# Numbers, gates and y rows of the gathered tokens placed through DRAM by GpSimd's queue, and expert transposes three pairs later

## The chip, the cores and the metric

The program runs on one core of a Trainium2 chip. The metric is the device time of one execution in microseconds, the median of several runs. The engines are TensorE (PE, matmuls; its weight loads are listed as PEld), VectorE (DVE), ScalarE (ACT), GpSimd (POOL) and SyncE (SP). Every engine takes its own queue of instructions in order. Transfers (DMA) are issued from the queues of SP, ACT or POOL and are carried out by 16 transfer engines that all issuers share.

## The reference

One decoder layer for 256 tokens of width 1024 in float32. First a mixer (linear attention and block-sparse attention, with a residual), then a retrieval of experts. The change touches only the second half:

```
xn = rmsnorm(x, norm2_w)
q  = (xn @ w_query).reshape(T, 8, 2, 128)            # 8 heads, two halves
s  = einsum('thpd,hpkd->thpk', q, subkeys)           # 128 keys per half
sv, si = top_k(s, 16)
cand    = sv[..., 0, :, None] + sv[..., 1, None, :]  # 256 candidates
top_s, pos = top_k(cand, 16)
expert  = take_along_axis(si0 * 128 + si1, pos)      # one of 16384
gate    = softmax(top_s)
act     = gelu(einsum('thkd,td->thk', u_tab[expert], xn))
out     = x + einsum('thk,thkd->td', gate * act, v_tab[expert])
```

Each token so has 8 x 16 = 128 experts, each with a row of 1024 floats in u_tab and one in v_tab.

## The kernel before

**Two ways for the experts.** The last 168 tokens ("many") go the dense way: TensorE multiplies their normed activations `yf` with the whole table u, 128 experts at a time (L120, 64 pairs `jp` of two pieces of 512 KB each), a gelu follows on ScalarE (L840), the gates are spread over all 16384 experts by products of one-hot rows (`one_hots`, `grid_group`, L808, from pair 31 on, `J0`), and TensorE multiplies with the whole table v (L881, again 64 pairs) into banks `acc`. The first 88 tokens ("few", `NS`) go by gathering: GpSimd's indirect transfer (L743) brings 128 rows of a table, one to each partition, and VectorE multiplies them with the token's normed row `y` and sums (L751, for u), or scales them by gate times gelu and adds them up in `ys` (L761, for v). There are 88 gathers from u and then 88 from v, through five buffers `rowsof`. A gather `k` takes its 128 row numbers from column `k` of the tile `ixs`.

**Three layouts.** `FEW = ((0, 64, 2), (64, 16, 8), (80, 8, 16))`: tokens 0 to 63 are spread over 2 blocks of 64 partitions each, tokens 64 to 79 over 8 blocks of 16, tokens 80 to 87 over 16 blocks of 8. So the y rows, the rstd, the expert numbers and the gates, which are computed with one token per partition, have to be copied to 2 + 8 + 16 = 26 places each. All these copies are transfers issued from ScalarE's queue, `parts_of` for numbers (`ixs`) and gates (`gs`), and the loop in `rows_of_few` for y rows (`ys`, L568) and rstd (`rs`, L569):

```python
for l, (t0, n, m) in enumerate(FEW):
    for b in range(m):
        nc.scalar.dma_start(ys[l][b * n:(b + 1) * n], rows_x2[t0:t0 + n])
        nc.scalar.dma_start(rs[b * n:(b + 1) * n, l:l + 1], rstd2[t0:t0 + n, 0:1])
```

**The stages.** From about 145 to 227 us TensorE computes the queries (16 pieces of w_query, L69 to L71, three matmuls each because each factor is split into two rounded parts). A piece comes by SP's queue into five `raw` buffers (L94), ScalarE rounds it (L100), VectorE computes the remainder (L101), and TensorE needs both; there are three buffers of each. In the same stage x2 is turned to rows (`x2_rows`), normed (`norm2`), and the y rows are placed (`rows_of_few`). From 227 us come the 64 pairs of u, then the 64 of v. Weight pieces are loaded ahead through a ring of 14 buffers.

**The order.** The search for the top 16 and what follows it is a list `work` of closures with costs, one list per half of the tokens. `work[0]` (tokens 0 to 127) is drained at 4.8 us of cost per pair, `work[1]` is spread over the pairs up to `J0 - 1`. What a closure leaves for TensorE, the transposes `turn` (L645) and `turn_gates` (L684), is put into `later` and issued in the next pair, behind its 16 matmuls. `few_to` spreads the 176 gathers over the pairs. This order of the program is not yet the order of the queues: the program is built with `schedule_with_timeline_sim=True` (L963), a planner that plays the program through with its own costs for operations and transfers, and puts an instruction into its engine's queue when its inputs are there in that plan. On the chip the order of each queue is then fixed. After pair 63 of v, L898 adds the residual to `acc`, L892 adds up the gathered sums `ys` on TensorE, and L893 adds their residual.

Of the kernel before, what the change touches and what calls it, by code (L numbers as in the profile page):

```python
# [9 lines left out]
F32 = mybir.dt.float32  # L10
# [8 lines left out]
D = 1024  # L19
# [6 lines left out]
J0 = 31  # L26
# [9 lines left out]
def layer(ctx: ExitStack, tc: tile.TileContext, a):  # L36
# [10 lines left out]
    def bank(tag):  # L47
        return psum.tile([128, 512], F32, name=tag, tag=tag, bufs=4 if tag == "sc" else 2)
# [464 lines left out]
    ixs = keep.tile([128, NS], U32, name="ixs")  # L513
    gs = keep.tile([128, NS], F32, name="gs")
    hs = keep.tile([128, NS], F32, name="hs")
    rs = keep.tile([128, 3], F32, name="rs")

    sums = act_p.tile([128, len(FEW), NS], F32, name="sums")
    gp.memset(sums, 0.0)
# [19 lines left out]
    spillT = nc.dram_tensor("x2_cols", (128, NC, ND), F32, kind="Internal").ap()  # L539
    rows_x2 = nc.dram_tensor("x2_rows", (NS, D), F32, kind="Internal").ap()  # L540

    def x2_rows(tt):
        x2 = tk.tile([128, D], F32, name="x2")
        for hf in range(2):
            p = bank("tr")
            for c in range(4):
                pe.transpose(p[:, c * 128:(c + 1) * 128], x2T[:, 4 * hf + c, tt * 128:(tt + 1) * 128], ident)
            ve.tensor_copy(x2[:, hf * 512:(hf + 1) * 512], p)
            junk = tk.tile([128, 512], BF, name="junk", tag="junk")
            sc_.activation(junk, x2[:, hf * 512:(hf + 1) * 512], AF.Square, accum_out=ss2[:, tt, hf:hf + 1])  # L550
        if tt == 0:
            nc.scalar.dma_start(rows_x2, x2[0:NS])
        gp.tensor_tensor(rstd2[:, tt:tt + 1], ss2[:, tt, 0:1], ss2[:, tt, 1:2], op=OP.add)

    def norm2():
        nc.scalar.dma_start(spillT, x2T[:, :, NS:])
        rstd_of(rstd2, D, NT)
        row = as_row(tk, rstd2, "rrow2")
        for c in range(NC):
            ve.scalar_tensor_tensor(yf[:, c], x2T[:, c, NS:], n2[:, c:c + 1], row[:, NS:], op0=OP.mult, op1=OP.mult)  # L560

    def rows_of_few():

        n2b = tk.tile([128, D], F32, name="x2")
        nc.scalar.dma_start(n2b, a["n2b"])
        for l, (t0, n, m) in enumerate(FEW):
            for b in range(m):
                nc.scalar.dma_start(ys[l][b * n:(b + 1) * n], rows_x2[t0:t0 + n])  # L568
                nc.scalar.dma_start(rs[b * n:(b + 1) * n, l:l + 1], rstd2[t0:t0 + n, 0:1])  # L569
            ve.scalar_tensor_tensor(ys[l], ys[l], rs[:, l:l + 1], n2b, op0=OP.mult, op1=OP.mult)  # L570


    scs = [tk.tile([128, NT, 4, 128], F32, name=f"scs{b4}") for b4 in range(4)]
# [4 lines left out]
    ij = tk.tile([128, 2, NT, 8, 16], F16, name="ij")  # L578
    cands = [tk.tile([128, 8, 112], F32, name="cand") for _ in range(NT)]
    later = []  # L580

    def top16(vals, idx, src):
        ve.max(vals[:, 0:8], src)
# [51 lines left out]
    def slots3(tt, w, eq):  # L635
        n = 8
        while n > 1:
            ve.tensor_tensor(eq[:, :, 0:n], eq[:, :, 0:n], eq[:, :, n:2 * n], op=OP.add)
            n //= 2
        ve.tensor_tensor(ij[:, w, tt], eq[:, :, 0], eq[:, :, 1], op=OP.add)  # L640
        later.append(lambda: turn(tt, w))

    def turn(tt, w):
        p = bank("tr").bitcast(F16)
        pe.transpose(p[:, :128], ij[:, w, tt].rearrange("p h k -> p (h k)"), identh)  # L645
        src, ts = many(tt, p)
        sc_.copy(idxT[:, w, ts], src[:, :, None].to_broadcast([128, ts.stop - ts.start, 2]))

    def parts_of(dst, src):

        for t0, n, m in FEW:
            w = SLOTS // m
            for b in range(m):
                nc.scalar.dma_start(dst[b * n:(b + 1) * n, t0:t0 + w], src[t0:t0 + n, b * w:(b + 1) * w])  # L654

    def experts():

        num = tk.tile([128, SLOTS], U32, name="num")
        r, c = (ij[:, w, 0].rearrange("p h k -> p (h k)") for w in range(2))
        numf = tk.tile([128, SLOTS], F32, name="numf")  # L660
        ve.scalar_tensor_tensor(numf, c, 128.0, r, op0=OP.mult, op1=OP.add)
        ve.tensor_copy(num, numf)
        parts_of(ixs, num)

    def gates(tt):
        gt = top[:, tt]
# [5 lines left out]
    def gates2(tt):  # L672
        gt = top[:, tt]
        sm = tk.tile([128, 8], F32, name="sm")
        ve.tensor_reduce(sm, gt, AX.X, OP.add)
        ve.reciprocal(sm, sm)
        ve.tensor_tensor(gt, gt, sm[:, :, None].to_broadcast([128, 8, 16]), op=OP.mult)
        if tt == 0:
            parts_of(gs, gt.rearrange("p h k -> p (h k)"))
        later.append(lambda: turn_gates(tt))  # L680

    def turn_gates(tt):
        p = bank("tr")
        pe.transpose(p[:, :128], top[:, tt].rearrange("p h k -> p (h k)"), ident)  # L684

        src, ts = many(tt, p)
        full = tk.tile([128, 128], F32, name="full")[:, :ts.stop - ts.start]
        g16 = tk.tile([128, 128], F16, name="g16")[:, :ts.stop - ts.start]
        sc_.activation(full, src, AF.Copy, scale=GS)
        sc_.copy(g16, full)  # L690
        sc_.copy(gf[:, 0, ts], g16)
        ve.tensor_tensor(gf[:, 1, ts], full, g16, op=OP.subtract)
# [128 lines left out]
    left1 = sum(c for c, _ in work[1])  # L821
    all1, spent = left1, 0.0
    for jp in range(64):
        pv = bank("mm")[:, :2 * ND].rearrange("p (k t) -> p k t", k=2)
        turns, later = later, []
        for k in range(2):
            by_col_whole(pv[:, k], take(("u", jp), k), yf)
        for f in turns:
            f()
        if jp == J0:  # L830
            assert not work[1] and not later
            tk_ctx.close()
            actB_p = ctx.enter_context(tc.tile_pool(name="actB", bufs=1))
            act[1] = actB_p.tile([128, 64, ND], F32, name="actB")
            oh = ctx.enter_context(tc.tile_pool(name="oh", bufs=2))
            one_hots(0)
        o = act_at(2 * jp, 2 * jp + 2)
        T = 4 * done_q
        if T < ND:
            sc_.activation(o[:, :, T:], pv[:, :, T:], AF.Gelu)  # L840
        if T:
            gl = oh.tile([128, 2, ND], F32, name="gl", bufs=1)
            sc_.activation(gl[:, :, :T], pv[:, :, :T], AF.Gelu)
            ve.tensor_tensor(o[:, :, :T], o[:, :, :T], gl[:, :, :T], op=OP.mult)
        if work[0]:
            spent -= 4.8
            while work[0] and spent < 0:
                c, f = work[0].pop(0)
                spent += c
                f()  # L850
            j1 = jp + 1
        else:
            few_to((jp - j1 + 1) * 2 * NS // (64 - j1 + 61))
            while work[1] and all1 - left1 < all1 * (jp + 1 - j1) / (J0 - 1 - j1):
                c, f = work[1].pop(0)
                left1 -= c
                f()
        while jp > J0 and done_q < NQ and done_q * (62 - J0) < (jp - J0) * NQ:
            grid_group(done_q, 2 * jp + 2)
            done_q += 1  # L860
            if done_q % 2 == 1 and done_q + 1 < NQ:
                one_hots(done_q + 1)
# [106 lines left out]
```

## Time and profile before

| what | value |
|---|---|
| median of 3 runs | 874.9 us (874.48 to 876.65) |
| the profiled execution | 877.12 us, span 875.3 us, mean granted clock 0.962 |
| busy | PE 823.0 us, DVE 482.1, ACT 247.3, POOL 215.1 |
| moved | 261.67 MB, mean 299 GB/s |
| chain that ended last | PE 82%, DVE 7%, DMA 5%, ACT's queue 3% |

The page gives the busy time of each engine, then 40 equal slices of the span with the busy share of each engine in tenths, the clock that TensorE was granted, and the traffic. Views of the trace give the same for any stretch of time, for one line of the program or one tile, and list who waited for whom. The span leaves out 1.8 us of the profiled execution's time.

### The profile page before, as it was taken

What the parts mean: (1) busy time and instruction counts of PE and PEld (TensorE: products, weight loads), DVE (VectorE), ACT (ScalarE), POOL (GpSimd) and SP (SyncE); (2) the same over time, 40 slices, a digit from 0 to 9 for tenths busy, and PEclk for the clock granted to TensorE, in tenths of its full rate; (3) what the DMA queues carried; (4) which work ended last, traced back from release to release, by engine and by line L of the source; (5) the groups of instructions that cost most, each with busy time, mean ns of one, the idle gap of its engine ahead of it and who ended that gap; (6) DMA issues with size and microseconds to landing.
All of it is one profiled execution on the core that took longest, in us unless ns stands there. A gap on an engine that the chain in (4) does not pass through costs nothing.

```text
span 875.3 us, 14841 instructions
## 1 busy us (share of the span) xinstructions
PE 823.0 (94%) x5734; PEld 777.0 (89%) x5734; DVE 482.1 (55%) x1060; ACT 247.3 (28%) x660; POOL 215.1 (25%) x252
## 2 busy tenths in 40 slices
PE   9999999928997499999999999999999999999995
PEld 6876689828997399999999999999999999999993
DVE  4795367494899644446666777645455445410003
ACT  5556345403220211019677776200000000000000
POOL 4141103000001833323222232433333333300000
PEclk9997899967999699999999999999999999999998
DMA  9453027814976899999999999999999999999701
GB/s 340 167 167 121 25 79 229 248 45 139 328 236 222 301 403 409 408 409 408 400 339 360 367 352 382 349 408 408 409 409 408 409 408 409 409 409 354 234 2 48
DMA packets 75551, 261.67 MB, mean 299 GB/s; under 512 B 10433, under 2 KB 12497, under 8 KB 75353
## 3 DMA queue, kind: packets, MB, share of 16 engines
q1 hardware_dynamic: 44883, 162.87, 50.0%
q0 software_dynamic: 25344, 92.29, 27.4%
q10 hardware_dynamic: 5254, 5.57, 2.3%
q8 instruction: 45, 0.74, 0.3%
q14 instruction: 25, 0.20, 0.1%
HBM read 258.50 MB, written 2.10 MB: 298 GB/s over the span
## 4 chain that ended last, share of the span: by engine, by line
PE 82%; DVE 7%; DMA 5%; ACTq 3%; ACT 1%; issue 1%; POOL 1%; SPq 0%; DVEq 0%
PE sc L881 31%; PE mm L120 28%; PE mm L71 4%; PE mm L69 4%; PE mm L70 4%; DMA raw<-in_v_rows 2%; PE tr L808 2%; ACTq L654 1%; PE sc L388 1%; ACTq L569 1%; PE mm L892 1%; ACTq L568 1%; DMA xT<-in_xT 1%; DMA ixs<-num 1%; PE sc L369 1%
## 5 line engine op out<-in xcount | busy, mean ns | idle before, releaser
L120 PE MATMUL mm<-yf,raw 128*128 128x168 f32 x1184 | 175.8, 307 | 0.0
L120 PEld LDWEIGHTS mm<-yf,raw 128*128 128x128 f32 x1184 | 169.5, 190 | 0.4 <-DMA raw<-in_u 0.4
L761 DVE SCALAR_TENSOR_TENSOR ys<-rowsof,hs,ys 128x1024 f32<-128x1024 f32 x85 | 109.1, 1284 | 101.6 <-DMA rowsof<-in_v_rows,ixs 101.4
L743 POOL DMA_INDIRECT rowsof<-in_u_rows,ixs x88 | 93.5, 1062 | 276.5 <-DVE hs L751 152.6
L751 DVE CUSTOM_DVE_ANT_0 junkd<-rowsof,ys 128x1024 bf16<-128x1024 f32 x88 | 107.5, 1222 | 48.8 <-DMA rowsof<-in_u_rows,ixs 47.9
L743 POOL DMA_INDIRECT rowsof<-in_v_rows,ixs x88 | 84.8, 964 | 147.2 <-DVE ys L761 125.7
L797 ACT ACTIVATE B<-E,gf 128x128 f16<-128x128 f16 x336 | 102.1, 388 | 22.3 <-PE tr L808 16.3
L881 PEld LDWEIGHTS sc<-actB,raw 128*128 128x128 f32 x608 | 87.1, 190 | 3.2 <-DMA raw<-in_v_rows 2.2
L881 PE MATMUL sc<-actB,raw 128*128 128x168 f32 x608 | 89.8, 307 | 0.1
L101 DVE TENSOR_TENSOR lo<-raw,hi 128x1024 fp32r<-128x1024 f32 x48 | 58.9, 1233 | 47.4 <-ACT hi L100 47.4
L881 PE MATMUL sc<-actA,raw 128*128 128x168 f32 x576 | 82.9, 306 | 0.0
L881 PEld LDWEIGHTS sc<-actA,raw 128*128 128x128 f32 x576 | 82.3, 190 | 0.0
L100 ACT ACTIVATE hi<-raw 128x1024 fp32r<-128x1024 f32 x48 | 50.4, 1057 | 67.2 <-PE mm L71 21.8
L120 PEld LDWEIGHTS mm<-yf,hi 128*128 128x128 f32 x432 | 63.3, 193 | 3.1 <-ACT actA L840 3.1
L120 PE MATMUL mm<-yf,hi 128*128 128x168 f32 x432 | 65.9, 311 | 0.1
L120 PE MATMUL mm<-yf,lo 128*128 128x168 f32 x432 | 64.8, 307 | 0.0
L120 PEld LDWEIGHTS mm<-yf,lo 128*128 128x128 f32 x432 | 62.1, 190 | 0.0
L69 PE MATMUL mm<-qhi,hi 128*128 128x256 f32 x128 | 38.7, 303 | 15.1 <-ACT hi L100 15.0
L898 DVE TENSOR_TENSOR x2d<-x2d,sc 128x504 f32<-128x504 f32 (+1 forms) x3 | 1.9, 619 | 91.1 <-PE sc L881 91.1
L840 ACT ACTIVATE actA<-mm 128x336 f32<-128x336 f32 x32 | 14.3, 450 | 105.3 <-PE mm L120 85.7
L71 PE MATMUL mm<-qhi,lo 128*128 128x256 f32 x128 | 38.6, 304 | 4.7 <-DVE lo L101 4.7
L69 PEld LDWEIGHTS mm<-qhi,hi 128*128 128x128 f32 x128 | 26.6, 208 | 15.6 <-ACT hi L100 15.6
(266 smaller groups left out, 1181.6 us busy)
## 6 DMA issues: line engine op xcount, KB each, us to landing
raw<-in_u SPq DMA_DIRECT2D x74, 512.0 KB
raw<-in_v_rows SPq DMA_DIRECT2D x74, 512.0 KB
hi<-in_u SPq DMA_DIRECT2D x27, 512.0 KB
lo<-in_u SPq DMA_DIRECT2D x27, 512.0 KB
hi<-in_v_rows SPq DMA_DIRECT2D x27, 512.0 KB
lo<-in_v_rows SPq DMA_DIRECT2D x27, 512.0 KB
raw<-in_w_rows SPq DMA_DIRECT2D x20, 512.0 KB
raw<-in_w_q SPq DMA_DIRECT2D x16, 512.0 KB
```

Of the source, the lines that this page charges most:

```text
L69: pe.matmul(ps, sh, mh, start=first, stop=False)
L70: pe.matmul(ps, sh, ml, start=False, stop=False)
L71: pe.matmul(ps, sl, mh, start=False, stop=last)
L100: sc_.activation(hi, raw, AF.Copy)
L101: ve.tensor_tensor(lo, raw, hi.bitcast(F32), op=OP.subtract)
L120: pe.matmul(ps, rv[:, c], mov[:, c], start=(c == 0), stop=(c == NC - 1))
L743: gp.indirect_dma_start(g, None, a[name], bass.IndirectOffsetOnAxis(ap=ixs[:, k:k + 1], axis=0))
L751: ve.tensor_tensor_reduce(junk, g, ys[place[k]], 1.0, 0.0, OP.mult, OP.add, hs[:, k:k + 1])
L761: ve.scalar_tensor_tensor(sumS, g, hs[:, k:k + 1], sumS, op0=OP.mult, op1=OP.add)
L797: sc_.activation(B[:, k], E[:, k], AF.Copy, scale=gf[:, m, 4 * q + k:4 * q + k + 1])
L808: pe.matmul(pv[:, k], A[:, k], B[m][:, k], start=(m == 0), stop=(m == 1))
L881: pe.matmul(acc[c // 3][:, c % 3], raw[:, c * 128:(c + 1) * 128], act[j // 64][:, j % 64], start=False, stop=j == NEXP - 1 and c in (2, 5, 7))
```

## The change

The y rows are scaled once, in token order (`yrow`), and `to_parts` writes them to DRAM and reads them back with one transfer per layout, three reads instead of 26 copies; the same for the numbers and the gates. All of these are issued by GpSimd's queue. The rstd column is no longer copied. The row copy of x2, its spill and the norm weights go from ScalarE's to SP's queue. The transposes of numbers and gates are due three pairs after the pair in which they are filed, and `work[1]` is spread over the pairs up to `J0 - 4`.

```diff
-    rs = keep.tile([128, 3], F32, name="rs")
+    xrow = tk.tile([128, D], F32, name="yrow")
     def x2_rows(tt):
-        x2 = tk.tile([128, D], F32, name="x2")
+        x2 = tk.tile([128, D], F32, name="x2") if tt else xrow
...
-            nc.scalar.dma_start(rows_x2, x2[0:NS])
+            nc.sync.dma_start(rows_x2, x2[0:NS])
     def norm2():
-        nc.scalar.dma_start(spillT, x2T[:, :, NS:])
+        nc.sync.dma_start(spillT, x2T[:, :, NS:])
+    def to_parts(dst, name, src, cols):
+        there = nc.dram_tensor(name, (NS, src.shape[1]), src.dtype, kind="Internal").ap()
+        gp.dma_start(there, src)
+        for l, (t0, n, m) in enumerate(FEW):
+            rows = there[t0:t0 + n]
+            if cols:
+                rows = rows.rearrange("t (m w) -> m t w", m=m)
+            else:
+                rows = rows[None].to_broadcast([m, n, src.shape[1]])
+            gp.dma_start(dst(l), rows)
+    def by_part(dst):
+        return lambda l: dst[:, FEW[l][0]:FEW[l][0] + FEW[l][1]]
     def rows_of_few():
         n2b = tk.tile([128, D], F32, name="x2")
-        nc.scalar.dma_start(n2b, a["n2b"])
-        for l, (t0, n, m) in enumerate(FEW):
-            for b in range(m):
-                nc.scalar.dma_start(ys[l][b * n:(b + 1) * n], rows_x2[t0:t0 + n])
-                nc.scalar.dma_start(rs[b * n:(b + 1) * n, l:l + 1], rstd2[t0:t0 + n, 0:1])
-            ve.scalar_tensor_tensor(ys[l], ys[l], rs[:, l:l + 1], n2b, op0=OP.mult, op1=OP.mult)
+        nc.sync.dma_start(n2b, a["n2b"])
+        yrow = xrow
+        ve.scalar_tensor_tensor(yrow[0:NS], xrow[0:NS], rstd2[0:NS, 0:1], n2b[0:NS], op0=OP.mult, op1=OP.mult)
+        to_parts(lambda l: ys[l], "y_rows", yrow[0:NS], False)
...
-        later.append(lambda: turn(tt, w))
+        later.append((at + 3, lambda: turn(tt, w)))
...
-        parts_of(ixs, num)
+        to_parts(by_part(ixs), "experts", num[0:NS], True)
...
-            parts_of(gs, gt.rearrange("p h k -> p (h k)"))
-        later.append(lambda: turn_gates(tt))
+            to_parts(by_part(gs), "gates", gt[0:NS].rearrange("p h k -> p (h k)"), True)
+        later.append((at + 3, lambda: turn_gates(tt)))
...
     for jp in range(64):
+        at = jp
-        turns, later = later, []
+        turns, later = [f for d, f in later if d <= jp], [x for x in later if x[0] > jp]
...
-            while work[1] and all1 - left1 < all1 * (jp + 1 - j1) / (J0 - 1 - j1):
+            while work[1] and all1 - left1 < all1 * (jp + 1 - j1) / (J0 - 4 - j1):
```

## Rows read from the trace of the kernel before

**Rows 1.** The page: busy time, TensorE in 40 slices, traffic in the same slices.

```profile
PE 823.0 (94%) x5734; PEld 777.0 (89%) x5734; DVE 482.1 (55%) x1060; ACT 247.3 (28%) x660; POOL 215.1 (25%) x252
...
PE   9999999928997499999999999999999999999995
...
GB/s 340 167 167 121 25 79 229 248 45 139 328 236 222 301 403 409 408 409 408 400 339 360 367 352 382 349 408 408 409 409 408 409 408 409 409 409 354 234 2 48
```

**Rows 2.** Windows: length, busy us (instructions) of PE, PEld, DVE, ACT, POOL; clock, DMA share, GB/s.

```profile
165.00:200.00 35.00, 14.77 (x99) 14.17 (x97) 26.24 (x141) 7.11 (x11) 0.00 (x0) 0.73 0.29 86
...
200.00:227.00 27.00, 26.14 (x192) 25.56 (x193) 16.87 (x59) 8.76 (x11) 0.00 (x0) 0.85 0.57 187
...
276.00:298.00 22.00, 5.07 (x33) 4.36 (x32) 16.58 (x25) 1.10 (x4) 14.21 (x10) 0.67 0.80 259
...
298.00:310.00 12.00, 12.00 (x77) 12.00 (x78) 8.11 (x16) 4.57 (x10) 8.41 (x8) 0.90 0.93 331
```

**Rows 3.** Waits of TensorE, 165 to 300 us: total, times, longest.

```profile
PE tr L645 <- ACT full L689: 16.4, 1, 16.4
...
PE mm L69 <- ACT hi L100: 15.0, 1, 15.0
...
PE mm L71 <- DVE lo L101: 4.7, 2, 4.0
...
PE tr L645 <- DVE ij L640: 1.1, 2, 0.7
```

**Rows 4.** ScalarE in order of time: start, length, what, count, idle before.

```profile
198.76 2.00 ACT L100 ACTIVATE hi<-raw 128x1024 fp32r<-128x1024 f32 x2 [12.77 <-DMA rs<-rstd]
...
278.01 17.06 ACTq L654 DMA_DIRECT2D ixs<-num  x24
```

**Rows 5.** Tiles rs, ys, ixs, issues: ns min/median/max, first and last start.

```profile
L569 ACTq DMA_DIRECT2D rs<-rstd x26: 497/638/708, 164.6 to 198.1; - x26
...
L568 ACTq DMA_DIRECT2D ys<-x_rows x26: 308/472/615, 158.6 to 197.6; - x26
...
L654 ACTq DMA_DIRECT2D ixs<-num x26: 537/632/675, 276.7 to 294.4; - x26
```

**Rows 6.** Windows of TensorE alone, busy us (instructions), clock, DMA, GB/s.

```profile
210.00:227.00 17.00, 17.00 (x148) 1.00 0.64 204
```

**Rows 7.** TensorE in order of time, behind the second hole.

```profile
297.72 3.89 PE L120 MATMUL mm<-yf,hi 128*128 128x168 f32 x16
...
301.45 7.00 PE L120 MATMUL mm<-yf,lo 128*128 128x168 f32 x48
```

**Rows 8.** GpSimd in order of time, the first and the third gather.

```profile
281.05 2.02 POOL L743 DMA_INDIRECT rowsof<-in_u_rows,ixs  x1 [117.07 <-PE tr L645]
...
285.40 0.94 POOL L743 DMA_INDIRECT rowsof<-in_u_rows,ixs  x1 [0.31 <-issue]
```

**Rows 9.** Chain of waits: two landings of small transfers.

```profile
198.07 1.75 DMA rs<-rstd
...
287.14 5.92 DMA ixs<-num
```

**Rows 10.** Windows of VectorE, lines L751 (287 to 391), L761 (550 to 875).

```profile
287.00:304.50 17.50, 12.32 (x20) 0.61 0.91 309
...
304.50:391.00 86.50, 38.24 (x62) 1.00 1.02 405
...
550.00:855.00 305.00, 105.29 (x82) 1.00 0.92 358
...
855.00:875.00 20.00, 3.84 (x3) 0.89 0.15 52
```

**Rows 11.** VectorE in order of time, 740 to 875 us.

```profile
768.67 1.28 DVE L761 SCALAR_TENSOR_TENSOR ys<-rowsof,hs,ys 128x1024 f32<-128x1024 f32 x1 [1.29 <-DMA rowsof<-in_v_rows,ixs]
...
860.89 0.68 DVE L898 TENSOR_TENSOR x2d<-x2d,sc 128x504 f32<-128x504 f32 x1 [90.94 <-PE sc L881]
...
862.34 1.28 DVE L761 SCALAR_TENSOR_TENSOR ys<-rowsof,hs,ys 128x1024 f32<-128x1024 f32 x1
```

More of the change, by code (lines that the diff above doesn't have):

```diff
@@ L580, in layer @@
     later = []
+    at = 0
     def top16(vals, idx, src):
@@ L647, in turn @@
         sc_.copy(idxT[:, w, ts], src[:, :, None].to_broadcast([128, ts.stop - ts.start, 2]))
[L649 to L654, printed above, removed]
     def experts():
```

## The prediction

> **What bounds the kernel now.** I read the page first. TensorE is busy 94% of the span, and its slices are full except for holes in the ninth, tenth, thirteenth and fourteenth slice, while the GB/s line stands near 409 from about 330 us on [rows 1]. So the end is set by TensorE's own work plus the holes in it; whoever fills a hole shortens the program by the hole, unless the tail gets longer. I cut the stretch around the holes into windows [rows 2]. From 165 to 200 us TensorE works 14.8 of 35 us; from 276 to 298 it works 5.1 of 22. In both the granted clock falls (0.73 and 0.67), and it is still 0.85 and 0.90 in the windows behind. The waits name who ends the long idles: an activation on ScalarE both times, L100 (the rounding of a weight piece) for 15.0 us and L689 (a copy of the gates) for 16.4 us [rows 3]. What ScalarE did meanwhile stands in the queue itself: L100 starts at 198.76 behind a row of transfers, and before L689 there is one block of 24 issues of ixs that lasts 17.06 us [rows 4]. Each of the small transfers costs ScalarE's queue 0.47 to 0.64 us, 26 times each for the rows, rstd and numbers [rows 5], and as often for the gates. The first hole is 52 issues, some 29 us of issue time spread over 158 to 199; the second is 26 of ixs and the last gs.
>
> **Part 1, rows and rstd off ScalarE.** Removed: 26 x 0.47 + 26 x 0.64 = 28.9 us of issues on ScalarE [rows 5], three multiplications of 1.28 us on VectorE become one, the rstd transfers go. Added: on SP three issues (x2 rows, spill, norm weights), which I take at the same 0.5 to 0.6 us each; they wait there for x2, and weight loads stand behind them, but up to five loaded pieces lie ahead of TensorE. On POOL one write and three reads. POOL has nothing else to do until 281 [rows 8], so nobody is behind them. What TensorE gets back: the 291 instructions of 165 to 227 [rows 2], at the pace of full clock in the last window, 17.00/148 = 0.115 us [rows 6], are 33.4 us of work in 62 us. So 28.6 us is the upper bound. The lower bound is the named idles alone, 15.0 + 4.7 = 19.7 us [rows 3], if the low clock stayed. I take 25: the slow matmuls come right after the idle and go with it, while VectorE, with 43 us of work in those 62, now has it in 37 and will make some pieces wait.
>
> **Part 2, numbers and gates off ScalarE, transposes three pairs later.** Removed: 52 issues x 0.63 us [rows 5]. The 16.4 us idle goes, and two small waits of the transposes for VectorE, 1.1 us together [rows 3], are covered by three pairs of matmuls. The slow start also goes: 16 matmuls took 3.73 us between their start and the next row, the next 48 took 7.00, or 0.146 each; 3.73 - 16 x 0.146 = 1.4 us [rows 7]. Sum 18.9; between zero (a new wait takes over) and 18.9 I take 18.5. What is late next is the placing: the first issue of the numbers goes at 276.7 [rows 5], the first gather starts at 281.05 [rows 8] after two issues and their landing. Now it is a write, its landing, a read, its landing. A direct POOL transfer does not occur before; its issue lies between 0 and the 2.02 us of an indirect one, I take the 0.94 of the plain case [rows 8]. A landing took 1.75 to 5.92 us [rows 9], I take 2.3, nearer to the small one on quiet queues. So 2 x (0.94 + 2.3) = 6.5 us after num against 4.3: the gathers start about 2 us later (bounds -1 and +12).
>
> A rule speaks against POOL as issuer. The first gather took 2.02 us in GpSimd's queue, the third 0.94 [rows 8]. The Trainium skill ("SBUF — State Buffer", section "SBUF: two separate sides") says that a VectorE operation in a two-port mode locks GpSimd out and so stops it from writing descriptors, and that transfers issued from ScalarE or SP do not suffer. The two durations would fit it, but these rows do not show what VectorE did at either. By it four issues in the chain cost up to 1.08 us more each, some 4 us, one or two multiplies more in the sum of part 3.
>
> **Part 3, what comes back at the end.** Each gathered block of expert rows is followed by one operation on VectorE. The order on VectorE was written by the planner, and it can be read. Three of the last multiplies (L761) stand behind the first output sum L898, which waits for TensorE's last matmul. On the chip the one before them started at 768.67, and then VectorE idles for 91 us; the three then run at 862 to 866.6 with TensorE finished, and the last products wait for them [rows 11]. So in the plan the gathered rows land later than on the chip; the plan is bound by transfers from the first gather on. The counts bear this out. By L751 (two instructions for each multiply) and L761, 10 multiplies fall in the second hole, 31 from there to 391, the other 47 of the 88 in the rest of the u stage, then 82 to 855 and 3 in the tail [rows 10]. VectorE was idle over half of the last long window (105.3 of 305 us), so a planner that held the rows to be there would have put them earlier. The hole was in the plan too, since ten multiplies stand ahead of the copy that ends it. In the hole the gathers had the transfer engines to themselves. Without it TensorE in the plan is at the same pair about 17 us sooner, the weight stream takes its share, and the plan is at every later pair about ten gathers behind, one more for the later start. Nothing in the plan makes that up until the weight stream ends. So I expect 3 + 11 = 14 multiplies behind L898. On the chip each costs 1.28 us if its row is there, as in the tail now [rows 11], and 17.5/10 = 1.75 us if row and operation take turns [rows 10]. Five buffers are full, so I take 1.4: 11 x 1.4 = 15.5 us longer tail. Bounds: 0 (the slip is made up) to 20 x 1.5 = 30 (it slips twice as far).
>
> **Sum.** -25 - 18.5 + 15.5 = -28 us. The profiled execution took 877.1 (span 875.3 and 1.8 around it), so 849; the median of the runs is 2.2 lower, so 847.
>
> **Rivals.**
> 1. The tail stays (three multiplies behind). For it: on the chip the gathers are 91 us early, and a planner that models transfers a little faster would move all of them ahead. Against: the counts above. Time: 847 - 15.5 = 831.
> 2. The gathers are late at the first one-hots. VectorE takes its queue in order, and 41 multiplies stand ahead of the gates and one-hots at 391 [rows 10]. If all stay there, 41 x 86.5/31 = 114 us from about 290 end at 404, while TensorE comes there 18 us before 391, 31 us too early at worst. Once TensorE waits, gathers take 1.75 us instead of 2.8, so I count half: 14 us, 861. Against: the planner, too, sees no hole and puts about ten fewer ahead.
> 3. The first hole is only half filled: SP holds the norm weights back until x2 is free, VectorE's scaled row waits for them, and rounding of pieces stands behind it. Gain 10 instead of 25: 862. For it: VectorE's L101 already ends 4.7 us of idles [rows 3].
> 4. Slower. The multiplies behind L898 in VectorE's queue decide: place, the tail; price, 1.4 us each. The 43.5 us gained are spent at 31 more, that is 34 behind L898, and past that the time is over 877. This needs the plan to reckon the DRAM round trip some 20 x 2.8 = 56 us longer than the old placing, since it gives away a gather per 2.8 us. Time at 38: 847 + 24 x 1.4 = 881. I see no row for it; the nearest landing is 5.92 [rows 9].
> 5. No change. The issue time of 17.06 us in one block [rows 4] is what the change moves, and if it were small against the transfers nothing would be gained: 875. The Trainium skill ("DMA: Bandwidth & Descriptors", section "Issuing engines are not separate DMA queues") says just this, that several issuers save only issue time, usually small beside the transfer. The trace disagrees here: with 0.2 to 16 KB each, the issue is the cost.
>
> **How the numbers follow.** Forecast 0.52; rival 1 0.22; rival 2 0.10; rival 3 0.08; rival 4 0.05; rival 5 0.03. A measurement of this kernel tells 0.3%, 2.6 us, from no change; so faster 0.92, same 0.03, slower 0.05. The forecast's own range, with 19.7 to 28.6 for part 1 and 8 to 17 multiplies in the tail, is 838 to 856. The range of 8 in 10 takes in rival 1 whole with 2 us below, 829, and the nearer half of rivals 2 and 3, to 862.
>
> **What would show it.** Part 1: L100's wait gone, TensorE idle under 5 us between 145 and the first u matmul, which starts near 202 and not 227; a granted clock near 1.0 there. Part 2: no idle over 1 us in the u stage before the one-hots; the first gather 6 to 9 us after num. Part 3: between 10 and 18 L761 behind the first L898, and 17 to 25 us from TensorE's last accumulation to its last product. Three there means rival 1; an idle of TensorE before L808 means rival 2; waits for DVE lo in the query stage mean rival 3. The forecast is wrong if the tail is as short as before, or if ScalarE's holes come back under another name.

## The result, and the profile after

The changed kernel takes 850.5 us (median of 4 runs, 848.89 to 852.24), the kernel before in the same comparison 875.8 us (4 runs, 874.48 to 878.48). The ratio is 0.9708, with a 95% interval of 0.9674 to 0.9742. The forecast was 847 us. The profiled execution took 849.4 us, of which the span covers 847.6.

The page after, the same three lines as in [rows 1].

```profile
PE 811.7 (96%) x5734; PEld 768.1 (91%) x5734; DVE 478.9 (57%) x1058; ACT 248.0 (29%) x660; POOL 224.5 (26%) x264
...
PE   8999999999999999999999999999999999999932
...
GB/s 341 182 154 145 26 75 215 265 229 368 233 218 338 408 409 408 408 406 369 356 357 373 360 351 381 409 409 409 408 409 409 408 409 409 408 345 200 1 191 173
```

TensorE's busy time is 11 us less for the same 5734 instructions, and the two pairs of holes are gone from its slices; in place of them the last two slices are low (3 and 2). The slice of 1 GB/s shortly before the end had its like before (2 GB/s); new is the traffic of 191 and 173 GB/s behind it: the transfers stand still while TensorE finishes, and then run again.

Two of the windows of [rows 2], and the tail (length; busy us and instructions of PE, PEld, DVE, ACT, POOL; clock, DMA share, GB/s).

```profile
165.00:200.00 35.00, 35.00 (x295) 35.00 (x294) 35.00 (x187) 13.42 (x18) 1.95 (x3) 1.00 0.84 240
...
276.00:298.00 22.00, 22.00 (x156) 22.00 (x155) 9.87 (x16) 2.26 (x5) 8.27 (x9) 1.00 1.03 409
...
811.50:847.60 36.10, 6.87 (x9) 1.82 (x8) 22.83 (x21) 0.00 (x0) 15.33 (x12) 0.64 0.63 214
```

TensorE now works all of 165 to 200 at a granted clock of 1.00, the 2.4 GHz level, on 295 instructions instead of 99, and all of 276 to 298. VectorE is full too in the first window. The tail, 36 us, has 9 instructions of TensorE.

Its waits after, to be laid beside [rows 3] (total, times, longest), and below them a wait of the kernel before that lies outside the window of [rows 3].

```profile
PE mm L901 <- DVE ys L769: 24.2, 2, 14.1
PE mm L120 <- DMA raw<-in_u: 1.5, 1, 1.5
...
PE sc L71 <- DVE lo L101: 0.8, 1, 0.8
...
PE mm L120 <- ACT actA L849: 0.7, 1, 0.7
```

```profile
PE mm L892 <- DVE ys L761: 4.3, 1, 4.3
```

L100 and the copy of the gates are gone from the list. The longest idle is now that of the last products (L901, L892 before) for VectorE's multiplies: 24.2 us in two pieces, where it was 4.3 in one.

GpSimd in order of time, after: the three placings, the first gathers, and gathers in the tail ([rows 5, 8] are before).

```profile
161.44 0.82 POOL L566 DMA_DIRECT2D y_rows<-yrow  x1 [5.36 <-DVE yrow L583]
165.70 1.95 POOL L573 DMA_DIRECT2D ys<-y_rows  x3 [3.44 <-DMA y_rows<-yrow]
...
247.15 0.55 POOL L566 DMA_DIRECT2D experts<-num  x1 [14.01 <-DVE num L670]
251.47 1.94 POOL L573 DMA_DIRECT2D ixs<-experts  x3 [3.77 <-DMA experts<-num]
257.74 1.09 POOL L751 DMA_INDIRECT rowsof<-in_u_rows,ixs  x1 [4.33 <-issue]
...
260.41 0.94 POOL L751 DMA_INDIRECT rowsof<-in_u_rows,ixs  x1 [0.30 <-issue]
...
814.49 1.86 POOL L751 DMA_INDIRECT rowsof<-in_v_rows,ixs  x1 [1.26 <-DVE ys L769]
...
824.51 2.04 POOL L751 DMA_INDIRECT rowsof<-in_v_rows,ixs  x1 [0.30 <-DMA rowsof<-in_v_rows,ixs]
...
830.98 0.94 POOL L751 DMA_INDIRECT rowsof<-in_v_rows,ixs  x1 [0.30 <-issue]
```

One write and three reads stand where 26 issues stood, each time. A write takes 0.55 to 0.82 us of the queue, a read some 0.65, and the reads start 3.4 to 3.8 us after the end of the write's issue.

TensorE in order of time, after: first matmul of u, first matmul of v, and the end.

```profile
194.72 3.58 PE L120 MATMUL mm<-yf,raw 128*128 128x168 f32 x24
...
512.60 5.58 PE L890 MATMUL sc<-actA,raw 128*128 128x168 f32 x38
...
806.81 4.72 PE L890 MATMUL sc<-actB,raw 128*128 128x168 f32 x32
825.62 3.37 PE L901 MATMUL mm<-ys,sums 128*88 128x512 f32 x4 [14.08 <-DVE ys L769]
839.08 3.46 PE L901 MATMUL mm<-ys,sums 128*88 128x512 f32 x4 [10.09 <-DVE ys L769]
```

VectorE in order of time, after, from the last multiply ahead of the output sums ([rows 11] before).

```profile
716.83 1.28 DVE L769 SCALAR_TENSOR_TENSOR ys<-rowsof,hs,ys 128x1024 f32<-128x1024 f32 x1 [1.26 <-DMA rowsof<-in_v_rows,ixs]
810.15 0.68 DVE L907 TENSOR_TENSOR x2d<-x2d,sc 128x504 f32<-128x504 f32 x1 [92.03 <-PE sc L890]
810.74 1.28 DVE L769 SCALAR_TENSOR_TENSOR ys<-rowsof,hs,ys 128x1024 f32<-128x1024 f32 x1
...
812.94 6.56 DVE L769 SCALAR_TENSOR_TENSOR ys<-rowsof,hs,ys 128x1024 f32<-128x1024 f32 x5
...
837.74 1.29 DVE L769 SCALAR_TENSOR_TENSOR ys<-rowsof,hs,ys 128x1024 f32<-128x1024 f32 x1 [1.12 <-DMA rowsof<-in_v_rows,ixs]
```

The residual sum L907 (L898 before) waits 92.03 us for TensorE, and 17 multiplies (16 of L769 and one of L771, the first of a half) stand behind it. They run from 810.74 to 839.03, and the last products wait. Five of their rows lay ready in the buffers; the other twelve gathers had to wait until those buffers came free, GpSimd's queue for 92.97 us.

Where the time went, from the spans: 875.3 before, 847.6 after.

| stretch | before | after | difference |
|---|---|---|---|
| start to the first matmul of u | 227.05 | 194.72 | -32.3 |
| u stage, to the first matmul of v | 334.9 | 317.9 | -17.0 |
| v stage, to the end of TensorE's last accumulation | 300.3 | 298.9 | -1.4 |
| tail, to the end of the span | 13.0 | 36.1 | +23.1 |

Of the first row 3.3 us are not the change's: the query stage begins that much earlier, because the granted clock between 70 and 100 us was 0.83 in this execution and 0.72 in the one of before, with the same instructions there. The profiles of the experiments show 0.72 to 0.83 there whatever part of the change they hold. The spans differ by 27.7 us and the medians by 25.2: the profiled execution of the kernel before was 1.3 us over its median, the one after 1.1 under.

### The profile page after: what moved, and what is told of

The parts are those of the page before. It is cut to its first block, busy times and chain, and to the rows that moved or that the text cites. A ratio compares the mean times of both kernels' runs of the same rounds, so it can differ in the third digit from the quotient of the medians.

```text
span 847.6 us, 14723 instructions
## 1 busy us (share of the span) xinstructions
PE 811.7 (96%) x5734; PEld 768.1 (91%) x5734; DVE 478.9 (57%) x1058; ACT 248.0 (29%) x660; POOL 224.5 (26%) x264
## 4 chain that ended last, share of the span: by engine, by line
PE 42%; DMA 23%; issue 17%; DVE 12%; POOL 3%; ACT 1%; SPq 0%; POOLq 0%; DVEq 0%; ACTq 0%
PE mm L120 25%; DMA rowsof<-in_v_rows,ixs 21%; PE mm L69 3%; PE mm L70 3%; PE mm L71 3%; POOL rowsof L751 3%; DVE ys L769 2%; PE tr L816 2%; DVE lo L101 1%; DMA rowsof<-in_u_rows,ixs 1%; DVE si L602 1%; PE sc L388 1%; DVE si L599 1%; DVE scs L600 1%; DVE sv L601 1%
## 5 line engine op out<-in xcount | busy, mean ns | idle before, releaser
L769 DVE SCALAR_TENSOR_TENSOR ys<-rowsof,hs,ys 128x1024 f32<-128x1024 f32 x85 | 109.2, 1285 | 97.3 <-DMA rowsof<-in_v_rows,ixs 97.1
L751 POOL DMA_INDIRECT rowsof<-in_v_rows,ixs x88 | 86.7, 985 | 223.2 <-DVE ys L769 209.4
L759 DVE CUSTOM_DVE_ANT_0 junkd<-rowsof,ys 128x1024 bf16<-128x1024 f32 x88 | 107.5, 1222 | 56.1 <-DMA rowsof<-in_u_rows,ixs 55.9
L751 POOL DMA_INDIRECT rowsof<-in_u_rows,ixs x88 | 87.9, 999 | 180.7 <-DVE hs L759 156.0
L101 DVE TENSOR_TENSOR lo<-raw,hi 128x1024 fp32r<-128x1024 f32 x48 | 58.9, 1230 | 32.6 <-ACT hi L100 32.5
L100 ACT ACTIVATE hi<-raw 128x1024 fp32r<-128x1024 f32 x48 | 50.7, 1059 | 55.1 <-PE mm L71 20.5
L907 DVE TENSOR_TENSOR x2d<-x2d,sc 128x504 f32<-128x504 f32 (+1 forms) x3 | 1.8, 618 | 92.0 <-PE sc L890 92.0
L849 ACT ACTIVATE actA<-mm 128x336 f32<-128x336 f32 x32 | 14.3, 449 | 105.4 <-PE mm L120 105.3
L70 PE MATMUL mm<-qlo,hi 128*128 128x256 f32 x128 | 36.1, 283 | 0.0
L71 PE MATMUL mm<-qhi,lo 128*128 128x256 f32 x128 | 36.0, 283 | 0.0
L69 PE MATMUL mm<-qhi,hi 128*128 128x256 f32 x128 | 35.9, 281 | 0.0
```

Of the source, the lines that this page charges most:

```text
L69: pe.matmul(ps, sh, mh, start=first, stop=False)
L70: pe.matmul(ps, sh, ml, start=False, stop=False)
L71: pe.matmul(ps, sl, mh, start=False, stop=last)
L100: sc_.activation(hi, raw, AF.Copy)
L101: ve.tensor_tensor(lo, raw, hi.bitcast(F32), op=OP.subtract)
L751: gp.indirect_dma_start(g, None, a[name], bass.IndirectOffsetOnAxis(ap=ixs[:, k:k + 1], axis=0))
```

## The experiments

The theory after the result: both holes gave back what the prediction said, the multiplies stranded in VectorE's queue took 23 us of it again, and only the order of that queue does this. Rivals: that the tail is long because the gathers really come late; that the second hole was worth nothing; that the issuer or the three pairs matter.

**Does the order make the tail?** `after_tail` and `before_tail` put the output sums behind the last multiply in VectorE's queue, in the changed kernel and in the one before:

```diff
-            ve.scalar_tensor_tensor(sumS, g, hs[:, k:k + 1], sumS, op0=OP.mult, op1=OP.add)
+            last[0] = ve.scalar_tensor_tensor(sumS, g, hs[:, k:k + 1], sumS, op0=OP.mult, op1=OP.add)
...
-        ve.tensor_tensor(x2d[:, cs], x2d[:, cs], acc[b][:, :cs.stop - cs.start], op=OP.add)
+        with tc.issue_after(last[0].ins):
+            ve.tensor_tensor(x2d[:, cs], x2d[:, cs], acc[b][:, :cs.stop - cs.start], op=OP.add)
```

> The changed kernel with one ordering edge more: the three output sums (L907) are queued behind the last multiply of the gathered rows, so that none of the 17 stands behind them. Theory (order of VectorE's queue): in the changed kernel TensorE ends at 811.5 us and the span at 847.6, 36 us later; 17 multiplies at 1.66 us fill 28 of them. With none behind, the tail is that of the kernel before less its three multiplies, 13.1 - 3.9 = 9 us. The 17 gathers then run in the v stage beside the weight stream, 17 x 2.56 = 44 us longer at 409 GB/s, where 16 matmuls take 2.55 instead of 2.28 us, so TensorE loses 4 to 5 us there. Sum 850.5 - 27 + 4.5 = 828 (824 to 833). Rival (the gathered rows really land late, the order only shows it): the same rows are waited for in another place, 845 to 851.

> The kernel before with the same ordering edge. Theory: three multiplies of 1.28 us leave the tail, 875 to 871 (870 to 873), all holes stay. Rival (rows late, or the edge itself saves something else): no change, 875, or more than 6 us saved.

Measured: `after_tail` 827.6 us (ratio 0.9459, 0.9429 to 0.9489), `before_tail` 868.1 us (0.9913, 0.9882 to 0.9944). VectorE at the end of `after_tail`, in order of time:

```profile
760.80 1.28 DVE L769 SCALAR_TENSOR_TENSOR ys<-rowsof,hs,ys 128x1024 f32<-128x1024 f32 x1 [1.28 <-DMA rowsof<-in_v_rows,ixs]
814.03 0.68 DVE L909 TENSOR_TENSOR x2d<-x2d,sc 128x504 f32<-128x504 f32 x1 [51.95 <-PE sc L891]
```

`after_tail` is where it was expected (824 to 833). The last multiply is done at 762, 52 us ahead of the output sum: the rows can all be there long before they are needed, and the stranding was the queue's order alone. The tail falls from 36 to 9 us. `before_tail` missed its expectation of 870 to 873: its 7.7 us lie with the rival, that the edge saves something else too. In the profiled executions the tail is 5.9 us shorter (13.0 to 7.1), since the wait of 4.3 us for the multiplies is gone and the last four products take 1.88 us instead of 3.27. The rest of the 8.8 us between those two spans is spread over the stages ahead (1.4 up to the first matmul of u, 0.6 in the u stage, 0.9 in the v stage), and its cause stays open.

TensorE in `after_tail`, in order of time, shows the cost in the v stage that the expectation put at 4 to 5 us.

```profile
664.49 18.40 PE L891 MATMUL sc<-actB,raw 128*128 128x168 f32 x128
...
697.08 20.47 PE L891 MATMUL sc<-actB,raw 128*128 128x168 f32 x128
...
815.26 3.60 PE L902 MATMUL mm<-ys,sums 128*88 128x512 f32 x8
```

128 matmuls take 18.40 us before the gathers leave the weights short (the first row), and 20.47 while the last of them run. The granted clock is 1.00 there too, the transfers are at 409 GB/s, and TensorE's weight loads wait 5.7 us for pieces between 690 and 770 us: the pieces come too late. The v stage is 301.4 us (514.01 to 815.42) against 298.9 in the changed kernel. So 27.6 us of tail are saved, the v stage is 2.5 longer for want of weights (starvation), and 1.4 were lost ahead of the v stage, where the edge changes nothing: the spans differ by 23.7.

**Which part strands the multiplies, and what is each part worth?** `p1` is the rows and rstd alone (numbers and gates as before), `p2` the numbers and gates with the three pairs alone (rows as before), `p2_old` the same without the three pairs. Against the changed kernel (in `p2` the x2 rows, spill and norm weights are issued by ScalarE again, as before):

```diff
 p1
-        to_parts(by_part(ixs), "experts", num[0:NS], True)
+        parts_of(ixs, num)
-            to_parts(by_part(gs), "gates", gt[0:NS].rearrange("p h k -> p (h k)"), True)
+            parts_of(gs, gt.rearrange("p h k -> p (h k)"))
-        later.append((at + 3, ...))
+        later.append((at + 1, ...))
-            while work[1] and all1 - left1 < all1 * (jp + 1 - j1) / (J0 - 4 - j1):
+            while work[1] and all1 - left1 < all1 * (jp + 1 - j1) / (J0 - 1 - j1):
 p2
...
-        to_parts(lambda l: ys[l], "y_rows", yrow[0:NS], False)
+        for l, (t0, n, m) in enumerate(FEW):
+            for b in range(m):
+                nc.scalar.dma_start(ys[l][b * n:(b + 1) * n], rows_x2[t0:t0 + n])
+                nc.scalar.dma_start(rs[b * n:(b + 1) * n, l:l + 1], rstd2[t0:t0 + n, 0:1])
 p2_old, on top of p2
-        later.append((at + 3, ...))
+        later.append((at + 1, ...))
-            while work[1] and all1 - left1 < all1 * (jp + 1 - j1) / (J0 - 4 - j1):
+            while work[1] and all1 - left1 < all1 * (jp + 1 - j1) / (J0 - 1 - j1):
```

> Part 1 alone: y rows through DRAM by GpSimd, row copy, spill and norm weights on SP; numbers and gates in 26 issues each from ScalarE as before, transposes due in the next pair as before. In its queue three multiplies stand behind the first output sum, as before the change. Theory: the first hole goes (29 us by the trace of the changed kernel, 25 as predicted), the second stays, the tail stays 13 us: 875.5 - 27 = 848 (845 to 851), as fast as the whole change. Rival (the tail grows because TensorE is earlier, whichever hole goes): tail 20 us or more, 856 or more.

> Part 2 alone: numbers and gates through DRAM by GpSimd, transposes three pairs later; y rows and rstd in 52 issues from ScalarE as before. In its queue 17 multiplies stand behind the first output sum. Theory: the second hole goes (17 us), the tail grows by 23 us as in the changed kernel: 875.5 - 17 + 23 = 881 (876 to 885), slower than before the change. Rival (each part saves its hole, the long tail needs both): 857 to 860.

> Numbers and gates placed by way of DRAM, issued by GpSimd, but the transposes due one pair later as before; rows and rstd as before. Theory: what puts the multiplies behind the first output sum is that the second hole is gone, not the three pairs. Then 17 multiplies stand there as with the three pairs, the tail is 36 us, and the time is 878 us (875 to 882). Rival: the three pairs shift the gathers in the queue; then the tail is near 13 us and the time near 855 us. A second rival, that the transposes wait without the three pairs: an idle of TensorE of 3 us or more before a transpose, 881 us or more.

Measured: `p1` 847.0 us (0.9689, 0.9653 to 0.9724), `p2` 878.5 us (1.0042, 1.0024 to 1.006), `p2_old` 877.9 us (1.0025, 1.0007 to 1.0043). All three are where they were expected. The first part alone is as fast as the whole change; the second alone is 0.4% slower than the kernel before. Waits of TensorE in `p1`, and VectorE at its end:

```profile
PE tr L660 <- ACT full L704: 16.4, 1, 16.4
```

```profile
829.85 0.68 DVE L914 TENSOR_TENSOR x2d<-x2d,sc 128x504 f32<-128x504 f32 x1 [89.95 <-PE sc L897]
830.45 1.28 DVE L776 SCALAR_TENSOR_TENSOR ys<-rowsof,hs,ys 128x1024 f32<-128x1024 f32 x1
...
832.65 2.60 DVE L776 SCALAR_TENSOR_TENSOR ys<-rowsof,hs,ys 128x1024 f32<-128x1024 f32 x2
```

The second hole stands as before (16.4 us), and three multiplies are behind the sum. The waits of `p2` and the end of its VectorE:

```profile
PE mm L903 <- DVE ys L771: 23.3, 2, 13.7
PE mm L69 <- ACT hi L100: 15.1, 2, 15.0
```

```profile
836.37 0.68 DVE L909 TENSOR_TENSOR x2d<-x2d,sc 128x504 f32<-128x504 f32 x1 [89.89 <-PE sc L892]
...
839.16 6.56 DVE L771 SCALAR_TENSOR_TENSOR ys<-rowsof,hs,ys 128x1024 f32<-128x1024 f32 x5
...
863.45 1.28 DVE L771 SCALAR_TENSOR_TENSOR ys<-rowsof,hs,ys 128x1024 f32<-128x1024 f32 x1 [0.55 <-DMA rowsof<-in_v_rows,ixs]
```

Here the first hole stands (15.0 us), the copy of the gates is gone, and 17 multiplies are behind the sum. `p2_old` has 17 too, and its waits of TensorE show 1.1 us for a transpose where the second rival wanted 3. So what strands the 14 is the placing of numbers and gates through DRAM, which closes the second hole, and neither the first part nor the three pairs.

VectorE's queue shows where the 14 are lost. Ahead of the first one-hot operation (L793, after the change L801) stand 41 multiplies for u before [rows 10] and 28 after (56 instructions of L759 up to 338 us), thirteen fewer; ahead of the last one-hot it is 85 and 72, thirteen fewer still. In `p1` the first number is 42, in `p2` 28, in `p2_old` 29, and in `actq_tail` (below), where ScalarE issues the same transfers, 28. So GpSimd as issuer does not strand them either. Whether in the plan it is the closed hole or the trip through DRAM was not taken apart.

`p1_tail` and `p2_tail` are the two with the edge.

```diff
 both, on top of p1 and p2
-        ve.tensor_tensor(x2d[:, cs], x2d[:, cs], acc[b][:, :cs.stop - cs.start], op=OP.add)
+        with tc.issue_after(last[0].ins):
+            ve.tensor_tensor(x2d[:, cs], x2d[:, cs], acc[b][:, :cs.stop - cs.start], op=OP.add)
```

> Part 1 alone with the ordering edge (no multiply behind the output sums). Theory: the edge takes the three multiplies and the slow start of the last products, 847 - 4 = 843 to 839; against the changed kernel with the edge (827.6) this shows what part 2 is worth once it costs no tail: the second hole of 17 us less the 4 to 5 us that the gathers then take from the weight stream, 12 us, so 840 (837 to 843). Rival (part 2 is worth nothing even so): 828.

> Part 2 alone with the ordering edge. Theory: only the first hole of 27 to 29 us is left in front of the changed kernel with the edge: 827.6 + 28 = 856 (852 to 859), 20 us faster than before the change where part 2 without the edge was 3 slower. Rival (the long tail comes from something else that part 2 does): 870 or more.

Measured: `p1_tail` 841.6 us (0.9604, 0.9568 to 0.964), `p2_tail` 852.6 us (0.9743, 0.9714 to 0.9772), both as expected. With the tail out of the way the parts can be summed: from `before_tail` at 868.1 the first gives 26.5, the second 15.5, together 42.0, and both in one kernel 40.5 (to 827.6).

**Do the three pairs and the issuer matter?** `due1_tail` has the edge and the old due pairs; `actq_tail` has the edge, and ScalarE issues the twelve transfers.

```diff
 due1_tail
-        later.append((at + 3, ...))
+        later.append((at + 1, ...))
-            while work[1] and all1 - left1 < all1 * (jp + 1 - j1) / (J0 - 4 - j1):
+            while work[1] and all1 - left1 < all1 * (jp + 1 - j1) / (J0 - 1 - j1):
 actq_tail
-        gp.dma_start(there, src)
+        nc.scalar.dma_start(there, src)
-            gp.dma_start(dst(l), rows)
+            nc.scalar.dma_start(dst(l), rows)
```

> The changed kernel with the ordering edge, transposes due in the next pair and the second list spread to J0 - 1, as before the change. Theory: the three pairs cover only the waits of the transposes for VectorE, 1.1 us in the kernel before: 827.6 + 1 = 829 (827 to 831). Rival (without them TensorE runs into VectorE, which now has 45 us of work in a stage that starts earlier): waits of TensorE for ij of 5 us or more, 833 or more.

> The changed kernel with the ordering edge, and its twelve transfers through DRAM issued by ScalarE instead of GpSimd. Theory (the number of issues made the holes, not the issuer): twelve issues of 0.6 us, but ScalarE now stands through the landing of each write, 3.5 us by the changed kernel's trace, before it can issue the reads; two banks of sums give TensorE about one pair, 4.6 us, of cover. So 828 to 832. Rival (GpSimd as issuer is what counts): holes of 5 us or more come back at the y rows, gates and numbers, 838 or more.

Measured: `due1_tail` 827.0 us (0.9452, 0.9425 to 0.9478), the same as with the three pairs: they are worth nothing that can be measured. `actq_tail` 832.2 us (0.9508, 0.9482 to 0.9534), at the upper end of the 828 to 832 expected and 4.6 us more than with GpSimd. So of the 40.5 us some 36 are there with ScalarE as issuer too: twelve issues in place of the many are most of the gain, and the issuer is the small rest. Its waits of TensorE, and those of SP's queue between 178 and 200 us:

```profile
PE mm L120 <- DMA raw<-in_u: 6.7, 1, 6.7
```

```profile
SPq L94 <- DMA ys<-y_rows: 12.9, 3, 8.4
```

TensorE waits 6.7 us for the first weight pieces of u, whose loads SP held back for a buffer, in a profiled execution (835.0) that is the slowest of the four. That the wait is named after the landing of the y rows, which no load needs, leaves open how ScalarE's queue brings it about; it was not tried further. That GpSimd is the better issuer here is shown, by 4.6 us; why is not.

**The starvation.** `tail_b4` and `tail_b3` are `after_tail` with four and three buffers for gathered rows instead of five; `after_b3` has three without the edge.

```diff
-        g = gat.tile([128, D], F32, name="rowsof", tag="rowsof")
+        g = gat.tile([128, D], F32, name="rowsof", tag="rowsof", bufs=3)
-            res = gat.tile([128, D], F32, name="res", tag="rowsof")
+            res = gat.tile([128, D], F32, name="res", tag="rowsof", bufs=3)
```

> The changed kernel with the ordering edge, four buffers for gathered rows instead of five. With the edge the gathers run beside the weight stream until 762 us though they are due at 811, and from 690 on TensorE loses 11%, some 7 us. Theory (fewer gathers under way leave more of the 409 GB/s to the weights): TensorE's loss shrinks by half or more, 824 (822 to 828). Rival (the share does not depend on how many gathers are under way, or VectorE now waits for each): no change, 827 to 829, or slower.

> The same with three buffers. Theory: the gathers slow down further, the weight stream is no longer short at all, 822 to 826, as long as the last multiply comes before TensorE's last matmul; if the gathers take over 3.4 us each they end after it and the tail returns, 830 or more. Rival (share independent of the number): 827 to 829.

> The whole change with three buffers for gathered rows in place of five, and no edge in the order. Theory: the plan holds the gathered rows up by transfers and not by buffers, so 17 multiplies stay behind the first output sum; TensorE's v stage is no longer short of weights, worth 1 to 5 us, and the tail loses up to 2 us since two rows fewer lie ready: 848 us (845 to 852). Rival: buffers set the plan; then the count goes up by five or more and the time is 856 us or more.

Measured: `tail_b4` 826.4 us (0.9434, 0.9401 to 0.9468), inside its 822 to 828, but TensorE's loss did not shrink by half: 128 matmuls still take up to 20.43 us, so the run tells nothing apart. `tail_b3` 821.0 us (0.9401, 0.9362 to 0.944), 1 us under its range and the fastest version here. TensorE and VectorE of `tail_b3`, in order of time:

```profile
698.33 18.40 PE L891 MATMUL sc<-actB,raw 128*128 128x168 f32 x128
...
730.25 18.40 PE L891 MATMUL sc<-actB,raw 128*128 128x168 f32 x128
...
809.48 3.60 PE L902 MATMUL mm<-ys,sums 128*88 128x512 f32 x8
```

```profile
808.39 1.28 DVE L769 SCALAR_TENSOR_TENSOR ys<-rowsof,hs,ys 128x1024 f32<-128x1024 f32 x1 [0.85 <-DMA rowsof<-in_v_rows,ixs]
809.59 1.68 DVE L909 TENSOR_TENSOR x2d<-x2d,sc 128x504 f32<-128x504 f32 x3
```

Every 128 matmuls take 18.40 now, and the last multiply ends as the last accumulation does: the gathers use the time up to the end instead of taking transfer time from the weights. The v stage is 293.7 us (515.93 to 809.64) instead of 301.4, the u stage 2.3 longer (319.6 against 317.3); the medians differ by 6.6.

`after_b3` missed its expectation: 860.5 us (0.9857, 0.9805 to 0.9908), 10 us more than with five buffers. VectorE at its end:

```profile
809.35 0.68 DVE L907 TENSOR_TENSOR x2d<-x2d,sc 128x504 f32<-128x504 f32 x1 [42.66 <-PE sc L890]
809.95 1.28 DVE L769 SCALAR_TENSOR_TENSOR ys<-rowsof,hs,ys 128x1024 f32<-128x1024 f32 x1
...
848.88 1.28 DVE L769 SCALAR_TENSOR_TENSOR ys<-rowsof,hs,ys 128x1024 f32<-128x1024 f32 x1 [1.41 <-DMA rowsof<-in_v_rows,ixs]
```

18 multiplies are behind the sum, one more than with five, so the buffers hardly set that count: the part of the theory on it holds. The time is the rival's (856 or more), but not for its reason (five more behind the sum). The price was wrong. From 809.95 to 850.17 it is 40.2 us, or 2.23 each. A gather takes 5.2 us (median) to land there; with the multiply 5.2 + 1.28 = 6.5 us in which a buffer is taken, over three buffers 2.2 us per row, and GpSimd's queue waits for a multiply ahead of most of these issues. So in the tail few buffers cost, where in the v stage they pay (293.7 us here too).

## Why the prediction was right, and where it was off

The three mechanisms that the prediction named are there: both holes close, and the multiplies move behind the first output sum. The sizes differ.

**Part 1** was 25, bounds 19.7 to 28.6. The trace has 32.3, less 3.3 for the front's clock: 29.0, 0.4 over the upper bound. The fear that VectorE would make pieces wait did not come true although it is busy all of 165 to 200: TensorE has no wait for L101 in the query stage any more (the 0.8 us of "sc L71" lie in the first 140 us). u begins at 194.72 instead of "near 202". `p1_tail` against `before_tail` gives 26.5.

**Part 2** was 18.5; the u stage is 17.0 shorter, and `p2_tail` against `before_tail` gives 15.5. The idle before the one-hots is gone as said; what is left in that stage is 1.5 us for a weight piece and 0.7 for L849, so the sign "no idle over 1 us" failed by half a us. The three pairs, which were to cover two small waits, cover nothing that can be measured. The placing takes longer than the 6.5 us assumed: from the issue of the numbers at 247.15 to the first gather at 257.74 it is 10.6 us. The issues were cheaper than the 0.94 taken (0.55 and 3 x 0.65), the waits for the landings longer than 2.3 (3.77 and 4.33). So the first gather is later than the 6 to 9 us that were named as a sign. This cost TensorE nothing, since rival 2 did not occur: no wait of TensorE for a one-hot is on its list.

The rule of the Trainium skill that spoke against GpSimd as issuer ("SBUF — State Buffer", section "SBUF: two separate sides") does not show in the chain: the four issues of the numbers took 0.55 + 1.94 us although VectorE was at work beside them, and the same transfers on ScalarE made the kernel 4.6 us slower. Whether any of VectorE's operations there was in a two-port mode no run shows. The same section of the Trainium skill has a second form of the lock: a VectorE operation with two inputs in SBUF against a GpSimd operation that reads SBUF. With this form the trace agrees in the tail. A multiply reads two tiles, `rowsof` and `ys`, and a gather's issue reads its row numbers from `ixs`. Nine of the twelve issues there began while a multiply ran; eight of them ended 0.81 to 0.82 us after that multiply did, the ninth 0.98. The three others took 0.94 us. One such pair, VectorE and GpSimd:

```profile
822.10 1.28 DVE L769 SCALAR_TENSOR_TENSOR ys<-rowsof,hs,ys 128x1024 f32<-128x1024 f32 x1 [0.79 <-DMA rowsof<-in_v_rows,ixs]
...
822.43 1.77 POOL L751 DMA_INDIRECT rowsof<-in_v_rows,ixs  x1 [0.30 <-issue]
```

The multiply ends at 823.38, the issue at 824.20. No run here took the lock away alone.

**Part 3** is the step that was mis-sized, with the mechanism right: the term "11 x 1.4 = 15.5". 14 multiplies more, not 11, stand behind the first sum, and each costs 28.3/17 = 1.66 us, not 1.4; so the tail is 23.1 us longer, not 15.5. Of the price, the landing is not the limit: 5.8 us (median) and 1.28 for the multiply over five buffers would be 1.42, the assumed value. GpSimd's queue is: the 11 issues from 814.49 to 830.98 come 16.49/10 = 1.65 us apart, 0.94 to 2.04 each with 0.30 between them. 4.05 of these 16.49 us are what the issues took over 0.94. As an estimate from these numbers, issues of 0.94 would come 1.24 apart, and the 1.42 of the five buffers would be the limit again: the price was taken too low by the holding of the issues. From the last accumulation to the last product it is 31 us, outside the 17 to 25 that were named. The argument for the count holds in the order of VectorE's queue: the slip is there at the first one-hot, and nothing makes it up to the last; but it is thirteen and not eleven, and one more at the end. That the plan is bound by transfers fits `after_b3`, whose count hardly depends on buffers, but the plan's own times were not looked at.

The sum: -28 was said, the spans give -27.7. It is closer than its terms, and that is luck: part 1 gave 4.0 more, and the v stage 1.4 and the front 3.3 us that the sum does not have, against 7.6 more in the tail and 1.5 less in part 2. By the medians the kernel gained 25.2, and the forecast of 847 is 3.5 us low. Two slips in its working carried nothing: with eight multiplies the low end of the forecast's own range is 835, not 838, and the traffic is not near 409 GB/s all the time from 330 us on, but 339 to 382 between 438 and 569 us.

Rival 1 (831, the tail stays) is what `after_tail` makes of the kernel, 827.6. Rivals 3 to 5 did not occur: L100's wait is gone, 17 and not 34 multiplies are behind the sum, and the issues were the cost. But rival 4's mechanism is real in the parts: `p2` alone, whose 15.5 us are eaten by the tail, is slower than before.

## What to carry to other kernels

When a queue's order is fixed by a planner, a hole that is closed elsewhere can strand work that is ready behind an instruction that waits for the end: list what stands behind the last big wait in each engine's queue, in the changed order, before the gain is booked. Here one ordering edge was worth 23 us, nearly as much as the change itself. And the number of buffers of a background stream can set its share of the transfers: three instead of five helped as soon as the stream had time to the end (four changed nothing clear of noise), and hurt while its rest lay bare in the tail.

## What the runs showed of the hardware

- A direct transfer costs GpSimd's queue 0.55 to 0.82 us for a write and 0.54 to 0.84 for a read, less than an indirect one (0.94 undisturbed). From the end of a write's issue to the first read it is 3.44 us for the y rows and 3.77 for the numbers, and from the end of the last read's issue to the first gather 4.33.
- An indirect issue that began while a multiply of two tiles ran on VectorE ended 0.81 us after that multiply (eight of nine in the tail) and took up to 2.04 us. The direct issues did not show this: the write of the numbers took 0.55 us, all of it beside one VectorE operation of 2.29 us with two inputs (L643).
- With transfers at 409 GB/s, five buffers in flight gave the gathers one block of 128 rows per 2.56 us, and TensorE's 128 matmuls took 11% longer (20.47 against 18.40 us, `after_tail`); with three it was a block per 2.9 us at 405 GB/s, and 18.40 us (`tail_b3`).
- The granted clock between 70 and 100 us was 0.72 to 0.83 from one profile to the next with the same instructions there (0.72 in the kernel before, in `after_tail` and in `p2`); between the two kernels compared this moved the start of the query stage by 3.3 us.
